# One decoder layer on one core: a norm factor spread later, one empty step ahead of a small product, a weight split moved into the last boundary loop, one more idle product

## The chip, the cores and the metric

The kernel runs on one core of a Trainium2 chip. Time is device microseconds (us) of one execution, the median over several runs. Below, PE is the matrix engine (TensorE), PEld its weight loads, DVE the vector engine, ACT the scalar engine, POOL GpSimd, and SP the engine that issues most of the transfers. The time before the change is 914.59 us, the median of 3 runs (913.2 to 915.72).

## The reference

One hybrid decoder layer over 512 tokens of width 1024, all in float32, in three sub-layers with a norm before and after each:

```
x = x + 0.5 * post1(swiglu1(pre1(x)))            # 1024 -> 2 x 2816 -> 1024
q, k, v, u = split(pre2(x) @ w_mix_in)           # 4 x 512 columns
a = dilated_attention(q, k, v)                   # 8 heads x 64
s = s5_mixer(u)                                  # 32 groups x 16 channels, 64 states
x = x + post2(concat(a, s) @ w_mix_out)
x = x + 0.5 * post3(swiglu2(pre3(x)))
```

`rms_norm` divides each token by the root of its mean square, so a sub-layer's first products can run on the unscaled input, and the factor r of each token is multiplied in when the product is read. The S5 mixer needs small parameter tensors that depend on the weights alone: powers of `a_bar`, `b_bar`, and short convolution kernels made from `b` and `c`.

## The kernel before, in words

**Tiling.** x and the hidden tensors lie transposed, channels on the 128 partitions and 512 tokens along the row. A weight tile of 128 x 1024 (512 KB) gives one product of a `[128, 1024]` block of weights with x: eight steps k over the 1024 channels. For precision every float32 operand is split into a high and a low part (`whi`, `wlo` of a weight, `xh`, `xl` of x), and each step is three matmuls of 512 columns (`mm3`). ACT makes the high part (a cast), DVE or POOL the low part (a subtraction). Weights go through three raw buffers (`wraw`) and four pairs of halves.

**Stages.** `run` chains ffn1 (span 0 to about 350), a boundary, mix (to about 600), a boundary, and ffn2. A boundary ends one sub-layer (its last products `yt`, the post norm, the residual) and starts the next (pre norm, and the first four products `first`), in two halves of 256 tokens each: the first loop over k prepares and multiplies half 0, the second half 1. `prep` makes y, x, `xh`, `xl` of one k and half on DVE and ACT, `begin` issues its 12 matmuls.

**ffn1.** Ahead of it PE runs five products of zeros (`idle`, plain float32, each as two matmuls). `products(f)` makes the gate and up products (`gu`) of block f, 24 matmuls each; `hidden(f)` reads them with r, applies silu and splits the result into `ah`, `al`. Blocks 0 to 7 are done so; `outp(0)` then multiplies them with the output weights (`yo`), of which the first two outputs m = 0 and 1 leave out the last block and take it up at the end. The factor r comes late: `sums` adds up squares with four tiny matmuls (`st`), DVE scales (`nv`), POOL takes the power (`r`), and `spread` copies r to all partitions with four matmuls against the identity (`rp`), which ACT copies to `rs`. The table `between` says at which k of which product this is issued.

**The parameters of S5 as a side job.** `ssm_params` is a generator. `step()` runs it to its next `yield`; the tables `other` and `between`, and `part` in `outp(0)`, call it after certain k, so its DVE, ACT and PE work is issued between the large products. Near its end it transposes `gb` in eight groups (`w1t`, four transposes each), copies each to a buffer `w1s` (ACT), and writes it to memory (`w1d`, SP); then makes `cz` (two tiles `pp`, cleared by POOL, filled by four ACT instructions at the line with `scale=1.0 - 2.0 * q`), then multiplies `cz` and `gb` into `kb` in two halves, copies that to `kt`, and transposes `kt` (`kc`). `gt`, `ut`, `w1s` and `kt` all come from one ring of four `[128, 512]` buffers.

**What sets the order.** Every engine runs its own list in order. The framework orders the list from the program's order and its own estimates; instructions through `self.fix` keep the program's order among themselves (all of PE's products here, most of DVE's in a boundary). A wait in front of an instruction holds up all behind it on its engine. SP issues transfers in order, and a load waits there until its buffer is free.

**`soon`.** `mix_soon` loads the weights of mix's first product and splits them into a room of its own, by one ACT cast and one DVE subtraction of 128 x 1024. The boundary calls it when it comes to the place `soon and k == ...`.

Of the kernel before, what the change touches and what calls it, by code (L numbers as in the profile page):

```python
# [17 lines left out]
P = 128  # L18
S = 512
D = 1024  # L20
KD = D // P
# [24 lines left out]
class Layer:  # L46
    def __init__(self, ctx, tc, a):
        self.tc, self.nc, self.a = tc, tc.nc, a
        pool = lambda n, b, **k: ctx.enter_context(tc.tile_pool(name=n, bufs=b, **k))
        self.cst = pool("cst", 1)  # L50
        self.big = pool("big", 6)
        self.wp = pool("wp", 2)
        self.tp = pool("tp", 4)
        self.sp = pool("sp", 2)
        self.ps = pool("ps", 8, space=PSUM)
        self.dr = pool("dr", 1, space=DRAM)
        nc = self.nc

        self.sw = self.tmp("sw")[:, :52 + P]
        nc.scalar.dma_start(out=self.sw, in_=a["smalls"])  # L60
        warm = self.tmp("warm")[:, :HT]
        nc.vector.memset(warm, 0.0)

        idle = self.bank("idle")
        for _ in range(5):
            self.mm(idle[:, :HT], lhsT=warm[:, :P], rhs=warm, start=True, stop=True)
        self.ident = self.cst.tile([P, P], F32, name="ident")
        make_identity(nc, self.ident)
        self.ones = self.cst.tile([P, 2], F32, name="ones")
        nc.vector.memset(self.ones, 1.0)  # L70
        self.mhalf = self.cst.tile([P, 4], F32, name="mhalf")
        nc.scalar.activation(out=self.mhalf, in_=self.ones[:, :1].to_broadcast([P, 4]), func=AF.Copy, scale=-0.5)
        self.mone = self.cst.tile([P, 4], F32, name="mone")
        nc.vector.memset(self.mone, -1.0)
        self.sm = self.cst.tile([P, 52], F32, name="sm")
        self.gh = self.cst.tile([P, 52], F32, name="gh")
# [78 lines left out]
    def fix(self, i):  # L155
        return self.tc.keep_in_program_order(i)
# [136 lines left out]
    def boundary(self, y, tail, ipost, half, inext, chunks, wide=None, soon=None):  # L293
# [40 lines left out]
        def prep(h, k, fix=lambda i: i):  # L334
            t = y(k)[:, hs[h]]
            xk = self.x(k)[:, hs[h]]
            fix(nc.vector.scalar_tensor_tensor(out=t, in0=t, scalar=self.g(ipost, k, half), in1=rr[h],
                                               op0=ALU.mult, op1=ALU.mult))
            fix(nc.vector.tensor_tensor(out=xk, in0=t, in1=xk, op=ALU.add))
            self.split(xh(k)[:, hs[h]], xl(k)[:, hs[h]], xk, self.g(inext, k), fix)  # L340
            if wide:
                fix(nc.scalar.activation(out=t, in_=xk, func=AF.Copy, scale=self.g(inext, k)))
            self.sq_acc(acc2[:, hs[h]], xk, k == 0, nc.gpsimd)

        def begin(h, k):
            for i in range(len(w)):
                self.mm3(o[i][:, hs[h]], w[i][0][:, k], w[i][1][:, k], xh(k)[:, hs[h]], xl(k)[:, hs[h]],
                         k == 0, k == KD - 1)
# [24 lines left out]
        late = []  # L373
# [18 lines left out]
        for k in range(KD):  # L392
            if k > 1:
                prep(0, k, fx if k > 5 else lambda i: i)
            begin(0, k)
            if soon and k == 2:
                soon()
            if k == 2:
                post[1][0](late, fix=fx)
            if k == 4:  # L400
                rr[1] = post[1][1]()
        for k in range(KD):
            prep(1, k)
            begin(1, k)
            if not wide and k == 3:
                pre[0][0](fixp=fx)
            if not wide and k == 6:
                pre[0][1]()
# [7 lines left out]
    def ffn(self, n, first, scope):  # L416
# [6 lines left out]
        o0, _, r, late = first  # L423
# [3 lines left out]
        nfirst = len(o)  # L427
# [3 lines left out]
        step = lambda: next(hook, None)  # L431
        other = {1: step, 3: step, 5: step}
        between = {(nfirst, 0): {}, (nfirst, 1): {}, (nfirst + 1, 0): {1: lambda: late[0](fixp=self.fix), 3: step, 5: step},
                   (nfirst + 1, 1): {1: late[1], 3: step, 5: step}}
        halves = iter([(f, i) for f in range(nfirst, NSTD[0]) for i in range(2)][len(self.ahead):])

        def ahead():
# [511 lines left out]
    def ssm_params(self, scope):  # L949
# [181 lines left out]
        czf = [t.rearrange("p n g c -> p n (g c)") for t in cz]  # L1131
        kt = self.tmp("kt")
        yield
        kb = self.bank("kb")
        for n4 in range(4):
            o = kb[:, n4 * P:(n4 + 1) * P]
# [98 lines left out]
    def mix_soon(self):  # L1235


        room = self.b16("soon", F32R).rearrange("p (i k) c -> p i (k c)", i=4)
        self.soon = self.load(self.a["wmi"][0], (KD, P), [room[:, 0], room[:, 1]])

    def mix_chunks(self):
        return [self.a["wmi"][c] for c in range(12, 16)]
# [398 lines left out]
```

## Time and profile before

| what | value |
|---|---|
| median of 3 runs | 914.59 us (913.2 to 915.72) |
| profiled execution, its own time | 914.35 us |
| its span, first to last instruction | 912.5 us |
| mean granted PE clock | 0.996 |
| busy: PE, DVE, ACT, POOL | 897.3, 663.1, 456.0, 217.1 us |
| bytes moved | 118.37 MB, mean 130 GB/s |

A row of the timeline gives the start in us, the duration, the engine, the line, the operation with output and inputs, and in brackets the idle time before it and what ended that. A matmul's duration is modelled to the end of its pipeline; how fast PE goes is read from the distance of two starts. Products of 512 columns start 0.227 us apart at full rate, those of 256 columns 0.114 us. Matmuls of plain float32 and transposes show as two records each.

### The profile page before, as it was taken

To read this page: it belongs to the slowest core of one execution; us is meant where nothing else is said; L and a number is where in the kernel's file an instruction comes from. 1 tells how busy PE (TensorE), PEld (TensorE's weight loads), DVE (VectorE), ACT (ScalarE), POOL (GpSimd) and SP (SyncE) were. 2 spreads that over 40 slices of the span, in tenths; PEclk is the share of its full clock that TensorE was granted. 3 is DMA by queue.
4 is the path that set the end of the run, shared out by engine and by line. 5 is a ranking of instruction groups with operands and counts; after the bars stand their busy time and mean duration, and the time that the engine had idled before them with its cause. 6 is when DMAs were issued, how large, how long until landed. Compare 5 with 4: busy or idle time off the path is not lost.

```text
span 912.5 us, 15703 instructions
## 1 busy us (share of the span) xinstructions
PE 897.3 (98%) x6314; PEld 807.0 (88%) x6314; DVE 663.1 (73%) x1065; ACT 456.0 (50%) x705; POOL 217.1 (24%) x130
## 2 busy tenths in 40 slices
PE   9999899999999999999999999999999999999996
PEld 7788688998899989988777789999899989998995
DVE  6998576765578565958989587996279658965966
ACT  7262573553355543535637465774456414541542
POOL 0253202342323224430000023513122212231211
PEclk9999999999999999999999999999999999999999
DMA  8224479664522153184221443363422412342322
GB/s 276 95 70 127 150 253 266 153 177 149 146 93 82 53 189 94 48 251 148 84 91 57 141 162 108 89 219 129 150 93 95 160 70 93 116 139 72 113 93 92
DMA packets 52760, 118.37 MB, mean 130 GB/s; under 512 B 8176, under 2 KB 11504, under 8 KB 52080
## 3 DMA queue, kind: packets, MB, share of 16 engines
q1 hardware_dynamic: 48928, 109.55, 36.5%
q0 software_dynamic: 2176, 4.19, 2.9%
q10 hardware_dynamic: 1584, 3.63, 1.1%
q8 instruction: 49, 0.80, 0.4%
q14 instruction: 23, 0.19, 0.1%
HBM read 107.66 MB, written 18.09 MB: 138 GB/s over the span
## 4 chain that ended last, share of the span: by engine, by line
PE 82%; DVE 11%; DMA 2%; issue 2%; ACT 2%; POOL 1%; SPq 0%; POOLq 0%; DVEq 0%; ACTq 0%
PE yo L164 22%; PE wx L164 20%; PE wq L164 10%; PE yt L164 6%; PE wy L164 5%; PE first L164 4%; PE prj L164 4%; PE prv L164 2%; DVE pp L964 2%; PE mo L164 2%; DVE wlo L139 2%; PE ys L164 1%; PE st L164 1%; DMA w1d<-w1s 1%; PE gl L164 1%
## 5 line engine op out<-in xcount | busy, mean ns | idle before, releaser
L137 ACT CAST whi<-wraw 128x1024 fp32r<-128x1024 f32 (+5 forms) x122 | 117.9, 971 | 139.3 <-PE yo L164 60.0
L139 POOL TENSOR_TENSOR wlo<-wraw,whi 128x1024 fp32r<-128x1024 f32 (+1 forms) x37 | 96.6, 2611 | 286.3 <-ACT whi L137 274.9
L139 DVE TENSOR_TENSOR wlo<-wraw,whi 128x1024 fp32r<-128x1024 f32 (+5 forms) x85 | 103.2, 1220 | 64.6 <-ACT whi L137 60.2
L164 PE MATMUL wx<-tq,whi 128*128 128x256 f32 (+1 forms) x817 | 141.6, 276 | 0.0
L164 PEld LDWEIGHTS wx<-tq,whi 128*128 128x128 f32 x817 | 122.8, 188 | 0.1
L139 DVE TENSOR_TENSOR wlo<-wsum,whi 128x1024 fp32r<-128x1024 f32 x68 | 82.8, 1219 | 48.4 <-ACT whi L137 48.4
L164 PE MATMUL wx<-tq,wlo 128*128 128x256 f32 x408 | 112.6, 276 | 0.0
L137 ACT CAST whi<-wsum 128x1024 fp32r<-128x1024 f32 x68 | 71.2, 1048 | 76.9 <-PE yo L164 25.8
L139 POOL TENSOR_TENSOR wlo<-wx,whi 128x1024 fp32r<-128x1024 f32 x16 | 46.1, 2882 | 197.3 <-ACT whi L137 161.4
L164 PEld LDWEIGHTS wx<-tq,wlo 128*128 128x128 f32 x408 | 76.6, 188 | 0.0
L164 PE MATMUL yo<-whi,ah 128*128 128x512 f32 x144 | 56.8, 395 | 0.0
L164 PE MATMUL yo<-whi,al 128*128 128x512 f32 x144 | 56.2, 390 | 0.0
L164 PE MATMUL yo<-ah,whi 128*128 128x512 f32 x144 | 56.1, 390 | 0.0
L164 PE MATMUL yo<-wlo,ah 128*128 128x512 f32 x144 | 56.1, 390 | 0.0
L164 PE MATMUL yo<-al,whi 128*128 128x512 f32 x144 | 56.1, 389 | 0.0
L164 PE MATMUL yo<-ah,wlo 128*128 128x512 f32 x144 | 56.0, 389 | 0.0
L164 PE MATMUL gu<-xh,whi 128*128 128x512 f32 x112 | 45.3, 405 | 0.0
L164 PE MATMUL gu<-xl,whi 128*128 128x512 f32 x112 | 44.1, 393 | 0.0
L164 PE MATMUL gu<-xh,wlo 128*128 128x512 f32 x112 | 44.0, 393 | 0.0
L164 PE MATMUL first<-xh,whi 128*128 128x256 f32 (+1 forms) x144 | 43.3, 300 | 0.6 <-ACT xh L186 0.6
L164 PE MATMUL first<-xl,whi 128*128 128x256 f32 (+1 forms) x144 | 43.3, 301 | 0.3 <-DVE xl L187 0.2
L164 PE MATMUL first<-xh,wlo 128*128 128x256 f32 (+1 forms) x144 | 42.3, 294 | 0.0
(310 smaller groups left out, 2499.3 us busy)
## 6 DMA issues: line engine op xcount, KB each, us to landing
wraw<-w1i SPq DMA_DIRECT2D x28, 512.0 KB, 3.9
wraw<-w2i SPq DMA_DIRECT2D x24, 512.0 KB, 3.6
wraw<-w2o SPq DMA_DIRECT2D x18, 512.0 KB, 4.5
wraw<-wmi SPq DMA_DIRECT2D x12, 512.0 KB, 4.0
wx<-w2i SPq DMA_DIRECT2D x10, 512.0 KB, 3.5
wraw<-w1o SPq DMA_DIRECT2D x8, 512.0 KB, 3.6
c<-w2i POOLq DMA_DIRECT2D x8, 512.0 KB, 7.6
wsum<-c SPq DMA_DIRECT2D x8, 512.0 KB, 4.2
```

The lines of the kernel that those rows point to most:

```text
L137: fix(self.nc.scalar.copy(out=hi, in_=raw))
L139: fix(eng.tensor_tensor(out=lo, in0=raw, in1=hi.bitcast(F32), op=ALU.subtract))
L164: i = self.nc.tensor.matmul(*a, **k)
L964: tt = lambda o, x, y, op: V.tensor_tensor(out=o, in0=x, in1=y, op=op)
```

## The change

Four edits:

- `between`: r is spread after k = 4 of the second product of block 2 in place of after k = 1, nine matmuls later, and that product calls one `step()` in place of two. So every later piece of `ssm_params` is issued one call later.
- `ssm_params`: one more empty `yield` ahead of `kb`, so `kb` and what follows are issued one further call later.
- `boundary` and `mix_soon`: `soon()` is called at k = 5 of the second loop in place of k = 2 of the first, and its two instructions now keep the program's order.
- `__init__`: a sixth idle product, of 128 columns.

```
         for _ in range(5):
             self.mm(idle[:, :HT], lhsT=warm[:, :P], rhs=warm, start=True, stop=True)
+        self.mm(idle[:, :P], lhsT=warm[:, :P], rhs=warm[:, :P], start=True, stop=True)
...
             if k > 1:
                 prep(0, k, fx if k > 5 else lambda i: i)
             begin(0, k)
-            if soon and k == 2:
-                soon()
...
         for k in range(KD):
             prep(1, k)
+            if soon and k == 5:
+                soon()
             begin(1, k)
...
-                   (nfirst + 1, 1): {1: late[1], 3: step, 5: step}}
+                   (nfirst + 1, 1): {4: late[1], 6: step}}
...
         kt = self.tmp("kt")
         yield
+        yield
         kb = self.bank("kb")
...
-        self.soon = self.load(self.a["wmi"][0], (KD, P), [room[:, 0], room[:, 1]])
+        self.soon = self.load(self.a["wmi"][0], (KD, P), [room[:, 0], room[:, 1]], fix=self.fix)
```

The order of PE around the first half of `kb` (`kb` is the output, `gb` and `pp104`, `pp105` the inputs; numbers count the tiles). Before:

```order
L164 MATMUL gu_1081<-xl_100,whi_1028 128x512
L164 MATMUL gu_1081<-xh_99,wlo_1029 128x512
L164 MATMUL kb_1088<-gb_703,pp104_1060 32x128 x4
L164 MATMUL kb_1088<-gb_704,pp105_1061 32x128 x4
L164 MATMUL gu_1081<-xh_99,whi_1028 128x512
```

and with the change:

```order
L165 MATMUL yo_1115<-al_249,whi_1068 128x512
L165 MATMUL yo_1115<-ah_248,wlo_1069 128x512
L165 MATMUL kb_1122<-gb_710,pp104_1080 32x128 x4
L165 MATMUL kb_1122<-gb_711,pp105_1081 32x128 x4
L165 MATMUL yo_1115<-ah_248,whi_1068 128x512
```

The half stood after k = 1 of the last `gu` product; it now stands after k = 1 of the first `yo` product, 24 matmuls of 512 columns further on.

The order of ACT from the weights of the first `yo` product to the copy `kt` (`w1s<-w1t` copy transposes out, `pp104` and `pp105` are `cz`, `gt` and `ah` belong to `hidden`). Before:

```order
L137 CAST whi_1076<-wraw_1075 128x1024
L1119 COPY w1s_990<-w1t_985 128x512
L1119 COPY w1s_1010<-w1t_1005 128x512
L456 ACTIVATE gt_1019<-gt_1019 128x512
L137 CAST whi_1203<-wraw_1202 128x1024
L183 CAST ah_247<-ut_1020 128x512
L1119 COPY w1s_1045<-w1t_1040 128x512
L1129 ACTIVATE pp104_1060<-pp4_341 64x16x16 x2
L1129 ACTIVATE pp105_1061<-pp4_341 64x16x16 x2
L137 CAST whi_1314<-wraw_1313 128x1024
L1143 COPY kt_1068<-kb_1088 128x512
```

and with the change:

```order
L138 CAST whi_1068<-wraw_1067 128x1024
L1130 ACTIVATE pp104_1080<-pp4_342 64x16x16 x2
L1130 ACTIVATE pp105_1081<-pp4_342 64x16x16 x2
L1120 COPY w1s_983<-w1t_978 128x512
L1120 COPY w1s_1003<-w1t_998 128x512
L457 ACTIVATE gt_1012<-gt_1012 128x512
L138 CAST whi_1172<-wraw_1171 128x1024
L184 CAST ah_248<-ut_1013 128x512
L1120 COPY w1s_1038<-w1t_1033 128x512
L1120 COPY w1s_1058<-w1t_1053 128x512
L138 CAST whi_1315<-wraw_1314 128x1024
L457 ACTIVATE gt_1107<-gt_1107 128x512
```

`cz` stood behind three copies to `w1s`; it now stands ahead of four. The copy to `kt` follows three rows after the last one shown.

The order of DVE around the subtraction for `soon` in the boundary from ffn1 to mix (`rp_3783` serves half 0 of the tokens, `rp_3956` and, with the change, `rp_3952` half 1; `nv_4093` and `nv_4089` are the first step of half 0's next norm factor). Before:

```order
L339 TENSOR_TENSOR x_98<-y_246,x_98 128x256
L139 TENSOR_TENSOR soon_3903<-wraw_3904,soon_3903 128x1024
L187 SCALAR_TENSOR_TENSOR xl_3587<-x_98,sm_96,xh_3586 128x256
L337 SCALAR_TENSOR_TENSOR y_246<-y_246,gh_97,rp_3783 128x256
L187 SCALAR_TENSOR_TENSOR xl_3587<-x_98,sm_96,xh_3586 128x256
```

and with the change:

```order
L338 SCALAR_TENSOR_TENSOR y_247<-y_247,gh_98,rp_3952 128x256
L340 TENSOR_TENSOR x_99<-y_247,x_99 128x256
L140 TENSOR_TENSOR soon_4118<-wraw_4119,soon_4118 128x1024
L188 SCALAR_TENSOR_TENSOR xl_3588<-x_99,sm_97,xh_3587 128x256
L226 TENSOR_SCALAR nv_4089<-st_4086 128x2
L188 SCALAR_TENSOR_TENSOR xl_3588<-x_99,sm_97,xh_3587 128x256
L226 TENSOR_SCALAR nv_4201<-st_4198 128x2
L140 TENSOR_TENSOR wlo_4230<-wraw_4228,whi_4229 128x1024
```

The subtraction left the middle of half 0's work and now stands ahead of the last two `xl` of half 1.

More of the change, by code (lines that the diff above doesn't have):

```diff
@@ L66, in __init__ @@
             self.mm(idle[:, :HT], lhsT=warm[:, :P], rhs=warm, start=True, stop=True)
+        self.mm(idle[:, :P], lhsT=warm[:, :P], rhs=warm[:, :P], start=True, stop=True)
         self.ident = self.cst.tile([P, P], F32, name="ident")
@@ L395, in boundary @@
             begin(0, k)
-            if soon and k == 2:
-                soon()
             if k == 2:
@@ L403, in boundary @@
             prep(1, k)
+            if soon and k == 5:
+                soon()
             begin(1, k)
@@ L433, in ffn @@
         between = {(nfirst, 0): {}, (nfirst, 1): {}, (nfirst + 1, 0): {1: lambda: late[0](fixp=self.fix), 3: step, 5: step},
-                   (nfirst + 1, 1): {1: late[1], 3: step, 5: step}}
+                   (nfirst + 1, 1): {4: late[1], 6: step}}
         halves = iter([(f, i) for f in range(nfirst, NSTD[0]) for i in range(2)][len(self.ahead):])
@@ L1133, in ssm_params @@
         yield
+        yield
         kb = self.bank("kb")
@@ L1238, in mix_soon @@
         room = self.b16("soon", F32R).rearrange("p (i k) c -> p i (k c)", i=4)
-        self.soon = self.load(self.a["wmi"][0], (KD, P), [room[:, 0], room[:, 1]])
+        self.soon = self.load(self.a["wmi"][0], (KD, P), [room[:, 0], room[:, 1]], fix=self.fix)
     def mix_chunks(self):
```

## The prediction

> **What bounds the kernel now.** I read the busy times first, then what PE waited for, then the timeline of PE around each wait, then the engines behind it.
>
> ```profile
> PE 897.3 (98%) x6314; PEld 807.0 (88%) x6314; DVE 663.1 (73%) x1065; ACT 456.0 (50%) x705; POOL 217.1 (24%) x130
> ```
>
> PE works without a break nearly everywhere, so an edit counts only by the idle time of PE that it removes or makes, or by the rate at which PE runs. The waits of PE, with total, count and longest in us:
>
> ```profile
> PE kb L164 <- issue: 2.3, 1, 2.3
> PE rp L164 <- POOL r L227: 1.6, 1, 1.6
> PE kb L164 <- ACT pp L1129: 0.5, 1, 0.5
> ```
>
> The change touches all three, and the start and the boundary, whose shorter gaps come below. The largest, in PE's timeline:
>
> ```profile
> 98.95 0.39 PE L164 MATMUL gu<-xh,wlo 128*128 128x512 f32 x1
> 101.61 0.43 PE L164 MATMUL kb<-gb,pp 128*32 128x128 f32 x8 [2.27 <-issue]
> 102.52 1.38 PE L164 MATMUL kb<-gb,pp 128*32 128x128 f32 x24 [0.48 <-ACT pp L1129]
> 103.84 0.80 PE L164 MATMUL gu<-xh,whi 128*128 128x512 f32 x1
> 107.85 1.08 PE L164 MATMUL kb<-gb,pp 128*32 128x128 f32 x32
> 108.86 0.50 PE L164 MATMUL gu<-xh,whi 128*128 128x512 f32 x1
> 110.35 0.40 PE L164 MATMUL yo<-ah,whi 128*128 128x512 f32 x1
> ```
>
> PE could have gone on at 99.18 (0.23 after the start of the last `gu`) and stands until 101.61. The name "issue" says that the trace saw no releaser; ACT's rows show one:
>
> ```profile
> 100.19 0.59 ACT L1119 COPY w1s<-w1t 128x512 f32<-128x512 f32 x1 [2.29 <-DMA w1d<-w1s]
> 100.67 1.71 ACT L1129 ACTIVATE pp<-pp 64x256 f32<-64x256 f32 x4
> ```
>
> ACT waited for a buffer of the ring until a `w1d` write had landed, and only then made `cz`: its first two instructions end near 101.5, where `kb` starts, the last two near 102.4, where the second part starts. The wait leaves a second loss, in the granted clock (the number before the DMA share):
>
> ```profile
> 102.00:103.00 1.00, 0.52 (x16) 0.51 (x17) 0.00 (x0) 0.98 (x2) 0.00 (x0) 0.86 0.96 363
> 103.00:106.00 3.00, 3.00 (x24) 2.23 (x16) 1.83 (x2) 0.45 (x1) 0.00 (x0) 0.50 0.41 96
> ```
>
> PE runs at 0.50 for about 3 us behind the gap.
>
> **kb: what the move is worth.** Standing: 103.84 - 99.18 = 4.66 us between products, of which a half of `kb` needs 1.01 when nothing is late (107.85 to 108.86), so 3.65 are lost. Half clock: the twelve products from 103.84 to 107.85 take 4.01, while six at full rate take 1.49 (108.86 to 110.35), twelve 2.98; 1.03 are lost. Together 4.7 us.
>
> Is the new place late enough? `kb` stands 24 products further on, 24 x 0.227 = 5.4 us. PE gets there at 99.18 + 5.4 - 1.5 (the gain of `rp`, below) = 103.1. Even in ACT's old order `cz` was done at 102.4. In the new one it precedes four `w1s` copies, so its limit is POOL's clearing:
>
> ```profile
> 90.45 0.99 POOL L1126 MEMSET pp<- 128x512 f32 x2
> ```
>
> 91.4 plus four times 0.43 gives 93.2: ten us of cover. What is late next? The four copies that `cz` overtook go through the ring; the last pair waits for the landing of the pair before.
>
> ```profile
> DMA to landing us min/median/max: 2.5/4.6/4.8
> ```
>
> By my estimate the pair after `cz` is copied by 94.3, lands by 99 (4.6 later), and the last pair is copied by 99.8. Behind it on ACT stand the weights of the third `yo` product (cast by 101, needed by PE at about 115), `gt` and `ah` of block 7, then `kt`. The last pair's write is queued on SP behind a load and lands at about 104.5, which frees the ring's slot for `kt`. The second half of `kb` ends on PE at about 106.4, `kt` is copied by 107.2, and `kc` stands 15 products behind, at 109.8: 2.6 us of cover. If that cover is gone, PE loses what is missing one for one. All eight accumulator banks that PE takes here were emptied at least 3 us earlier in this reckoning. Bounds of the term: 0 (the wait moves along) to 4.7. I take 4.7, since every cover that I can name is positive.
>
> **rp.**
>
> ```profile
> 37.93 0.39 PE L164 MATMUL gu<-xh,wlo 128*128 128x512 f32 x1
> 39.88 1.16 PE L164 MATMUL rp<-ident,r 128*128 128x128 f32 x8 [1.57 <-POOL r L227]
> 38.79 1.03 POOL L227 TENSOR_TENSOR r<-nv,mhalf 128x4 f32<-128x4 f32 x1 [3.67 <-DVE pp L964]
> ```
>
> POOL has r at 39.82. Nine products more are 9 x 0.227 = 2.04 us, so PE wants r at 38.16 + 2.04 = 40.20 and no longer waits: 1.57 at most in this execution, with 0.3 of cover. `rs` is then some 0.5 us later, and DVE places six more `ssm_params` instructions ahead of the first `gt`:
>
> ```profile
> 44.89 1.09 DVE L964 TENSOR_TENSOR pp<-pp,pp 128x256 f32<-128x256 f32 x3
> 45.89 0.68 DVE L455 TENSOR_TENSOR gt<-first,rs 128x512 f32<-128x512 f32 x1
> ```
>
> At 1.09 for three, `gt` goes from 45.9 to about 48. It frees accumulators that block 4 takes 66 products after `rp`, at about 54 by my estimate (39.9 + 66 x 0.227 is 54.9, less what PE gains). Nothing waits. The one `step()` fewer changes places, not work. I take 1.5; bounds 0 to 2.04.
>
> **soon.** Half 0 of the boundary is where DVE is behind PE:
>
> ```profile
> 366.56 1.04 ACT L137 CAST soon<-wraw 128x1024 fp32r<-128x1024 f32 x1
> 368.68 1.21 DVE L139 TENSOR_TENSOR soon<-wraw,soon 128x1024 fp32r<-128x1024 f32 x1
> 373.44 0.28 PE L164 MATMUL first<-xh,wlo 128*128 128x256 f32 x1
> 373.87 0.71 PE L164 MATMUL rp<-ident,p 128*128 128x128 f32 x4
> 377.16 0.28 PE L164 MATMUL first<-xh,whi 128*128 128x256 f32 x1
> 377.57 0.39 PE L164 MATMUL first<-xl,whi 128*128 128x256 f32 x1
> 378.98 0.38 PE L164 MATMUL first<-xh,whi 128*128 128x256 f32 x1
> 379.56 0.38 PE L164 MATMUL first<-xl,whi 128*128 128x256 f32 x1 [0.20 <-DVE xl L187]
> ```
>
> Three steps from product to product are 0.43, 0.41 and 0.58 in place of 0.114: 0.32 + 0.30 + 0.47 = 1.1 us. The 1.21 us on DVE ahead of them go away, so all three can. At the new place, DVE and PE stood so:
>
> ```profile
> 386.23 0.48 DVE L187 SCALAR_TENSOR_TENSOR xl<-x,sm,xh 128x256 fp32r<-128x256 f32 x1
> 388.40 0.28 PE L164 MATMUL first<-xl,whi 128*128 128x256 f32 x1
> 387.62 0.48 DVE L187 SCALAR_TENSOR_TENSOR xl<-x,sm,xh 128x256 fp32r<-128x256 f32 x1 [0.58 <-ACT xh L186]
> 389.70 0.38 PE L164 MATMUL rp<-ident,r 128*128 128x128 f32 x2
> ```
>
> `xl` of k = 6 was 1.7 us ahead of its product. DVE gains about as much as PE, and 1.21 now stand in between: 0.0 to 0.5 of cover. The load behind `soon` on SP, so far issued at 369.93 as its buffer came free, now goes at about 386.5, and its cast stood at 396.48, so about 6 us remain after 4 of landing.
>
> ```profile
> 369.93 0.33 SPq L143 DMA_DIRECT2D wraw<-wmi  x1
> 396.48 1.05 ACT L137 CAST whi<-wraw 128x1024 fp32r<-128x1024 f32 x1
> ```
>
> I take 0.9; bounds -0.5 (the 1.21 stand in the way after all, less the small cover, and only part is regained) to 1.1.
>
> **The idle product.**
>
> ```profile
> 1.22 4.64 PE L164 MATMUL idle<-warm 128*128 128x256 f32 x10 [1.22 <-DVE pp L972]
> 6.47 0.80 PE L164 MATMUL first<-xh,whi 128*128 128x512 f32 x1 [0.61 <-ACT xh L186]
> 9.98 0.63 PE L164 MATMUL first<-xl,whi 128*128 128x512 f32 x1
> 11.18 0.39 PE L164 MATMUL first<-xh,wlo 128*128 128x512 f32 x1
> ```
>
> Ten matmuls of 256 columns take 4.64, two of 128 about 0.46; they end by 6.3 inside the gap of 0.61, so they cost nothing. The first products stand 0.43 apart until about 10.4 and 0.227 from there: half rate. A shorter gap may end this sooner, by up to nine products x 0.2 = 1.8 us, but then PE only meets r at 39.82 again; at most 0.3 is left over. I take 0.
>
> [...]
>
> **The sum.** 4.7 + 1.5 + 0.9 + 0 = 7.1 us. The profiled execution took 914.35, its span 912.5, and lies 0.2 under the median of 914.59. Span 905.4, execution 907.25, median 907.5: 0.8% faster. Less than 0.3% (2.7 us) can hardly be told from no change here.
>
> **The rivals.**
>
> *The start gets longer (chance 0.10).* The wait at `rp` hid up to 1.57 us of a slow start; without it a start whose half-rate spell is 3 us longer, as long as the spell at `kb`, costs seven products x 0.2 = 1.4. For it: 0.3 of cover is all that is left. Against: the idle product works the other way. 908.9. [...]
>
> *The wait was not for cz (0.07).* The trace says "issue" for 2.27. If PE stood there for a reason of its own, it stands at the new place too, with the half clock behind it: 7.1 - 3.65 - 1.03 = 2.4 gained, 912.2. Against: `cz` ends within 0.1 us of both starts.
>
> *The ring decides, a little (0.06) or wholly (0.04).* `kt` needs the slot of the last `w1s` pair. From a `kt` more than 2.6 us late, PE waits at `kc`. One round trip of 4.6 late gives 2.0 of wait, and 1 more if the clock halves: 909.5 to 910.5. To be slower than before takes three round trips, 13.8 late: 11.2 of wait and 1 of half clock against 7.1 gained, 919.7. For it: before, ACT and DVE both stood for `w1d` writes here. Against: ring use at each `hidden` is lower now, since two copies less stand ahead of block 5's.
>
> *soon only moves its wait (0.05).* 1.2 us at k = 6 and 7 in place of the 1.1 removed: no gain here, 908.4 to 908.9.
>
> *The forecast (0.68).* Its own range, with noise of about 0.7 us as in the three runs, is 906 to 909.
>
> The lower end of all is 4.7 + 2.04 + 1.1 = 7.8, 906.8, less 1 of noise: 905.8. The upper end takes in the short ring case: 910.5. Faster: 0.68 + 0.10 + 0.06 + 0.05 = 0.89; within 0.3%: 0.07; slower: 0.04.
>
> **What would show it.** In the changed profile: no wait at `kb`, and the granted clock at 1.00 from 99 to 107; no wait at `rp` of block 2, or one under 0.3; steps between `first` products in the boundary all near 0.114 at k = 6 and 7 of half 0 and k = 0 of half 1; PE busy still about 897 in a span near 905. The prediction is wrong if a wait stands at `kc` or at a `yo` product's weights, if the half clock returns, or if PE waits for `xl` at k = 6 or 7 of half 1.

## The result, and the profile after

The changed kernel takes 910.53 us, the median of 22 executions (906.28 to 914.98), against 913.58 for the kernel before in 22 executions beside it: a ratio of 0.9962, with a 95% interval of 0.9948 to 0.9976. That is 3.0 us less, where 7.1 were forecast. The median is of little use here, since the 22 times fall into two groups: ten from 906.3 to 908.3, where the forecast of 907.5 lies, and twelve from 910.2 to 915.0. The profiled execution, 911.97 with a span of 910.1, is of the upper group.

PE's busy time and its longest waits in the changed kernel, with total, count and longest in us:

```profile
PE 896.8 (99%) x6316; PEld 808.4 (89%) x6316; DVE 668.8 (73%) x1065; ACT 455.6 (50%) x705; POOL 215.3 (24%) x130
```

```profile
PE wx L165 <- DVE kp L720: 2.6, 1, 2.6
...
PE rp L165 <- POOL r L228: 0.2, 1, 0.2
```

Both rows of `kb` are gone, and of the wait at `rp` 0.2 is left. Where PE stood and then ran at 0.50 before, and in half 0 of the boundary, the busy times by stretch now read as follows (PE's busy time is the second number; the granted clock stands ahead of the last two):

```profile
101.00:104.00 3.00, 3.00 (x41) 2.20 (x40) 2.90 (x4) 1.73 (x3) 0.00 (x0) 1.00 0.89 307
104.00:107.00 3.00, 3.00 (x41) 2.22 (x40) 1.37 (x3) 0.59 (x1) 1.49 (x1) 1.00 0.95 305
...
370.00:390.00 20.00, 20.00 (x147) 18.51 (x146) 12.86 (x26) 10.16 (x21) 9.46 (x11) 1.00 0.53 165
```

So the places that the change aimed at do what was forecast. Matching the products of the two traces in their order shows how far the changed kernel is ahead at the same product (start before, less start after; the value that holds behind the place named):

| behind | ahead by, us |
|---|---|
| the tenth product | 1.5 |
| `rp` of block 2 | 2.8 |
| `kb` and `kc` | 7.4 |
| half 0 of the boundary | 8.9 |
| mix | 7.8 |
| the stall at 784.87, its first product | 5.1 |
| the same stall, six us later | 3.3 |
| the last product | 2.6 |

What is new is one stall in the last stage. PE's timeline, and the stretches behind it:

```profile
782.05 0.28 PE L165 MATMUL wq<-xh,wlo 128*128 128x256 f32 x1
784.87 0.50 PE L165 MATMUL wx<-tq,whi 128*128 128x256 f32 x2 [2.55 <-DVE kp L720]
```

```profile
785.00:787.00 2.00, 2.00 (x11) 2.00 (x12) 1.97 (x3) 0.29 (x1) 0.00 (x0) 0.59 0.74 242
787.00:789.00 2.00, 2.00 (x13) 2.00 (x12) 1.49 (x2) 0.77 (x1) 0.00 (x0) 0.56 0.08 29
```

PE stands for 2.55 us and then runs near half clock for almost 4. By the table this costs 7.8 - 3.3 = 4.5 us, and about so far apart are the medians of the two groups, 907.7 and 912.1. The rows of SP, DVE and POOL tell how it comes about. In this stage a `pair` of blocks takes seven block products; DVE forms sums of weight blocks (the additions at L654) and splits them (L140), and POOL splits two blocks of each pair, `h12 = cut(a12, True)` and `cut(a22, True)`. The timeline of SP, DVE and POOL in the changed kernel:

```profile
768.86 0.37 SPq L624 DMA_DIRECT2D wsum<-w2i  x1
770.02 0.34 SPq L144 DMA_DIRECT2D wraw<-w2o  x1
...
774.06 1.23 DVE L654 TENSOR_TENSOR wsum<-wraw,wsum 128x1024 f32<-128x1024 f32 x1 [1.22 <-DMA wsum<-w2i]
...
775.27 3.41 POOL L140 TENSOR_TENSOR wlo<-wx,whi 128x1024 fp32r<-128x1024 f32 x1 [11.26 <-ACT whi L138]
...
776.34 4.56 DVE L654 TENSOR_TENSOR wsum<-wsum,wx 128x1024 f32<-128x1024 f32 x2
...
780.65 2.48 POOL L140 TENSOR_TENSOR wlo<-wraw,whi 128x1024 fp32r<-128x1024 f32 x1 [1.97 <-ACT whi L138]
...
780.82 3.40 DVE L140 TENSOR_TENSOR wlo<-wraw,whi 128x1024 fp32r<-128x1024 f32 x1
784.14 0.68 DVE L720 TENSOR_TENSOR kp<-wx,kp 128x512 f32<-128x512 f32 x1
```

The load of 768.86 landed late, so DVE began its first addition 1.22 late. Two additions then met POOL's first split and took 4.56; where they start ahead of it (below) they take 2.35. The next split of DVE started 0.17 behind POOL's second one and took 3.40 in place of 1.22. `kp`, the addition that frees the accumulators `wx` that PE wants, came after it.

### The profile page after: what moved, and what is told of

The parts are those of the page before. It is cut to its first block, busy times and chain, and to the rows that moved or that the text cites. A ratio compares the mean times of both kernels' runs of the same rounds, so it can differ in the third digit from the quotient of the medians.

```text
span 910.1 us, 15705 instructions
## 1 busy us (share of the span) xinstructions
PE 896.8 (99%) x6316; PEld 808.4 (89%) x6316; DVE 668.8 (73%) x1065; ACT 455.6 (50%) x705; POOL 215.3 (24%) x130
## 4 chain that ended last, share of the span: by engine, by line
PE 88%; DVE 5%; ACT 1%; issue 1%; POOLq 0%; POOL 0%; DVEq 0%; ACTq 0%
PE yo L165 22%; PE wx L165 21%; PE wq L165 10%; PE gu L165 6%; PE yt L165 6%; PE wy L165 5%; PE prj L165 4%; PE first L165 4%; PE prv L165 2%; PE mo L165 2%; PE ys L165 1%; PE st L165 1%; PE gl L165 1%; PE pt L1225 1%; PE sc L165 1%
## 5 line engine op out<-in xcount | busy, mean ns | idle before, releaser
L140 POOL TENSOR_TENSOR wlo<-wraw,whi 128x1024 fp32r<-128x1024 f32 (+1 forms) x37 | 96.0, 2595 | 284.4 <-ACT whi L138 260.0
L165 PE MATMUL wx<-tq,whi 128*128 128x256 f32 (+1 forms) x817 | 143.6, 279 | 2.6 <-DVE kp L720 2.6
L140 DVE TENSOR_TENSOR wlo<-wraw,whi 128x1024 fp32r<-128x1024 f32 (+5 forms) x85 | 103.3, 1222 | 55.4 <-ACT whi L138 52.4
L140 DVE TENSOR_TENSOR wlo<-wsum,whi 128x1024 fp32r<-128x1024 f32 x68 | 82.9, 1220 | 44.1 <-ACT whi L138 44.1
L140 POOL TENSOR_TENSOR wlo<-wx,whi 128x1024 fp32r<-128x1024 f32 x16 | 45.6, 2847 | 202.0 <-ACT whi L138 189.9
L654 DVE TENSOR_TENSOR wsum<-wsum,wx 128x1024 f32<-128x1024 f32 x23 | 42.4, 1872 | 0.2
```

The costliest lines, as they stand in the source:

```text
L140: fix(eng.tensor_tensor(out=lo, in0=raw, in1=hi.bitcast(F32), op=ALU.subtract))
L165: i = self.nc.tensor.matmul(*a, **k)
L654: add = lambda x, z, t: V.tensor_tensor(out=t, in0=x, in1=z, op=ALU.add)
```

## The experiments

Twelve runs were made (one repeats the changed kernel, and the kernel without the idle matmul was run twice), in three groups, each group on one chip beside runs of the kernel before, whose median was 914.62, 913.27 and 913.40. Times are medians in us; ratios are to the kernel before, with a 95% interval.

### The changed kernel again, and the four ways to change the stall

**Once more**, with no edit.

> The changed kernel once more. Up to 780 us its trace is 7.8 us ahead of the one before; at 784.87 PE stands for 2.55 us (wx behind DVE's kp) and then runs at half clock for about 4 us, and ends only 2.4 ahead. Theory A (one late load): in that execution the w2i load of a wsum buffer landed 5.1 us after its issue, where the others take 3.5 to 3.8; DVE's add started 1.2 late and DVE's next split then met POOL's split and took 3.40 us in place of 1.22. Then the stall comes and goes from execution to execution: the times fall into two groups, about 907.5 without it and 911 to 913 with it, and a profile near 907.5 shows no wait at kp. Rival B (a place that is always short now): every execution has a wait at that place, and the two groups come from something else, so a profile near 907.5 would show the wait as well. Rival C: the groups come from the half-rate spell at the beginning, some 2 us longer or shorter; then a slow execution has its first full-rate product near 10 us and a fast one near 7.

910.40 (906.84 to 911.73, six executions; 0.9945, 0.9925 to 0.9964): 906.84 and 907.50 on one side, 909.53 to 911.73 on the other. The profile, of 911.27, has the stall again (PE waits 2.7 behind `kp`), again behind a late load (5.2 us). Its half-rate spell at the beginning ended at 7.4, as in the first profile of the upper group (7.3), which rules out C. A profile of an execution of the lower group was not obtained for this kernel, so A is not separated from B by this run alone.

**Without POOL in the pairs:**

```
- h12 = cut(a12, True)
+ h12 = cut(a12)
- times(X, h22 if ahead else cut(a22, True), tq[2], False)
+ times(X, h22 if ahead else cut(a22), tq[2], False)
```

> The changed kernel with both splits of each pair that POOL does (a12 and a22) done by DVE. DVE gets some 2.4 us more work per pair of 19 us, and never works beside POOL there. Theory A (the stall is the meeting of DVE and POOL behind a late load): no stall is left even where the load is late, DVE's splits and adds all take 1.22 us, and the times are one group near 907.5. Rival B (DVE is simply short of time there, whoever it meets): with more work on DVE the stall is as long or longer, in more executions, 911 to 915. Rival D (a late load is enough by itself): two groups as before.

907.88 (907.18 to 909.34, five executions; 0.9926, 0.9912 to 0.9940): one group. In its trace the same load is later than ever (5.9 us), DVE's timeline shows a wait of 2.00 for it, and yet:

```profile
775.46 1.22 DVE L654 TENSOR_TENSOR wsum<-wraw,wsum 128x1024 f32<-128x1024 f32 x1 [2.00 <-DMA wsum<-w2i]
...
781.14 1.22 DVE L140 TENSOR_TENSOR wlo<-wraw,whi 128x1024 fp32r<-128x1024 f32 x1
```

PE's waits in that kernel:

```profile
PE wx L165 <- DVE kp L720: 0.3, 1, 0.3
```

Every one of DVE's splits and additions takes 1.22 and PE waits 0.3. So a late load alone does not stall PE, nor does more work on DVE; the meeting with POOL is needed. B and D fall.

**Without the added idle matmul:**

```
- self.mm(idle[:, :P], lhsT=warm[:, :P], rhs=warm[:, :P], start=True, stop=True)
```

> The changed kernel without its added idle matmul (five of 512 columns are left). Counted by products, the changed kernel's trace is 1.5 us ahead by the tenth product, since its half-rate spell ends near 7.3 us in place of 10.4, and r comes 0.7 earlier. Theory I (the idle matmul closes the gap ahead of the first product, and the clock therefore rises earlier): without it the spell lasts to about 10.4 again, and the kernel takes 0.7 to 1.5 us more, 908.2 to 909 without the stall. Rival (the spell's end moves by itself from execution to execution): the median stays at about 907.5 without the stall, and the spell's end is not bound to this edit.

The five that are left have 256 columns each, not 512. 907.86 (907.12 to 909.59, five executions; 0.9921, 0.9907 to 0.9936): faster than the changed kernel, and no stall. Theory I falls: the half-rate spell ended at 7.3 without the idle matmul as well. The kernel with the empty step alone, which has no sixth idle matmul either, also had it end at 7.2. Of all the traces only the one before had a spell to 10.4.

Why no stall? The timeline of SP, DVE and POOL at the same pair:

```profile
770.76 0.37 SPq L623 DMA_DIRECT2D wsum<-w2i  x1
...
774.65 1.22 DVE L653 TENSOR_TENSOR wsum<-wraw,wsum 128x1024 f32<-128x1024 f32 x1
...
776.92 2.35 DVE L653 TENSOR_TENSOR wsum<-wsum,wx 128x1024 f32<-128x1024 f32 x2
...
777.18 4.36 POOL L139 TENSOR_TENSOR wlo<-wx,whi 128x1024 fp32r<-128x1024 f32 x1 [11.26 <-ACT whi L137]
...
779.84 2.78 DVE L139 TENSOR_TENSOR wlo<-wraw,whi 128x1024 fp32r<-128x1024 f32 x1 [0.56 <-ACT whi L137]
...
782.56 2.40 POOL L139 TENSOR_TENSOR wlo<-wraw,whi 128x1024 fp32r<-128x1024 f32 x1 [1.03 <-ACT whi L137]
```

DVE's additions started ahead of POOL's split, kept their 2.35, and POOL's took 4.36. The load was not late. What the transfer engines did in the 3.5 us behind the issue of that load (packets, MB and share of the 16 engines' time for each queue, and the load's us to landing), first in the changed kernel:

```profile
q1 hardware_dynamic: 309, 0.69, 57.4%
q8 instruction: 1, 0.02, 1.8%
...
wsum<-w2i SPq DMA_DIRECT2D x1, 512.0 KB, 5.1
```

and in the kernel without the idle matmul:

```profile
q1 hardware_dynamic: 304, 0.66, 56.3%
...
wsum<-w2i SPq DMA_DIRECT2D x1, 512.0 KB, 3.6
```

One packet of 16 KB of instructions, which takes about 1 us (0.88 to 1.45 over the 49 of the changed kernel's trace), stands among the load's packets in the one and not in the other. Between such fetches PE runs 111 to 147 matmuls in the changed kernel's last stage, 127.6 in the mean of eleven, each with its weight load; the list of packets in the trace gives their times. The whole trace has 49 of them for 6316 matmuls and as many weight loads, 258 to a packet and near the 255 of the last stage (2 x 127.6), so they are taken for PE's; the trace does not name the engine. No wait of PE in this stage is put down to a fetch, but the load with such a packet among its own landed after 5.1 us, the one without after 3.6. The added idle product is two matmul records (6316 in place of 6314; the transposes show as one record each, `w1t` as 32 for 32), so by this estimate every later packet is fetched two records earlier in PE's work. This is called theory F in the expectations that follow.

The fourteen traces bear F out at this pair, with one point left open. In all of them the load is issued at the same place of PE's work, behind 5406 matmuls without the idle ones. In the five traces with 10 idle records the fetch starts 3.5 to 5.7 us behind the issue, and the load lands after 3.5 or 3.6; in the seven traces with 12 records it starts 1.2 to 3.4 behind, and the load lands after 3.9 to 5.9. That point is the size: two records of 256 columns are only 0.23 us of PE's work, two steps of 0.114. Counted in all of PE's matmul records, idle ones too, this fetch never starts before the 5427th. In three traces (the two with 22 idle records and the one with 12 and no POOL in the pairs) it starts there or two records on, in the others up to 39 records later. Why a difference of 0.23 in when it could start so often decides whether it falls among the load's packets or behind them was not shown.

**The same, a second time.**

> The changed kernel without its added idle matmul, a second time: its five executions so far were 907.1 to 909.6, none with the stall, where the changed kernel has it in about half of 28. Theory F (two records fewer leave the fetch behind the load): no execution above 910. Rival (chance: five of five at one half has 3%): about half of them at 911 to 913.

907.02 (905.63 to 908.57, five executions; 0.9930, 0.9915 to 0.9945). Ten of ten executions without the idle matmul are below 910, and its second profile shows no wait at `kp`.

**As many records, no added work:**

```
- for _ in range(5):
+ for _ in range(4):
      self.mm(idle[:, :HT], lhsT=warm[:, :P], rhs=warm, start=True, stop=True)
- self.mm(idle[:, :P], lhsT=warm[:, :P], rhs=warm[:, :P], start=True, stop=True)
+ for _ in range(2):
+     self.mm(idle[:, :P], lhsT=warm[:, :P], rhs=warm[:, :P], start=True, stop=True)
```

> The changed kernel with the idle matmul taken away again and one of the five of 256 columns cut into two of 128: the columns of the kernel without it, but 12 matmul records ahead of the first product, as many as in the changed kernel. Theory F (the number of records sets where the 16 KB fetch falls against the w2i load): the fetch runs 2.5 to 3.1 us behind that load's issue, and the stall is back in about half of the executions: two groups, 907.5 and 911 to 913, median 909 to 911. Rival (the added work or the shorter gap at the beginning was the cause): one group at 907.0 to 907.9, as in the two kernels without the idle matmul, and the fetch 4.4 or more behind the load.

910.45 (906.33 to 913.13, twelve executions; 0.9957, 0.9939 to 0.9975), in two groups again: five from 906.3 to 908.5, seven from 910.2 to 913.1. Its profile (913.13) has the fetch 3.4 behind the issue (2.5 to 3.1 were expected), the load landing after 5.5 us, and the stall. PE's longest waits there:

```profile
PE wx L166 <- DVE kp L721: 2.9, 1, 2.9
PE rp L166 <- POOL r L229: 1.8, 1, 1.8
```

The columns are those of the kernel without the idle matmul; only the records differ. F holds in that the records decide, and the work or the gap at the beginning is not the cause.

**Ten records more:**

```
- for _ in range(5):
-     self.mm(idle[:, :HT], lhsT=warm[:, :P], rhs=warm, start=True, stop=True)
- self.mm(idle[:, :P], lhsT=warm[:, :P], rhs=warm[:, :P], start=True, stop=True)
+ for _ in range(11):
+     self.mm(idle[:, :P], lhsT=warm[:, :P], rhs=warm[:, :P], start=True, stop=True)
```

> The changed kernel with its idle matmuls in eleven pieces of 128 columns in place of five of 256 and one of 128: the same columns less nothing and the same 4.7 us of work ahead of the first product, but 22 matmul records in place of 12. Theory F: PE's instructions are fetched in pieces of 16 KB, a piece for about 128 matmuls with their weight loads, so ten more records ahead bring every later fetch 1.1 us earlier against the work. In the two stalled traces the fetch (about 1 us on one transfer engine) ran 2.5 to 3.1 us behind the issue of the late w2i load, in the traces without the stall 4.4 to 4.7 behind it, after the load had landed. With the fetch due ahead of the load's packets, the load lands in 3.5 to 3.8 again and the times are one group near 907.5. Rival (the load is late for another reason): two groups, 907.5 and 911 to 913, as in the changed kernel.

911.90 (909.09 to 914.57, twelve executions; 0.9983, 0.9971 to 0.9995). The number that was expected is missed: there is no group at 907.5. The stall has left its place, as F said, but stands at another. At the old pair the fetch now falls at 773.05, 0.15 behind the issue of the load at 772.90. That load still lands after 4.7, so the step of the expectation that such a fetch is harmless is wrong too, but no stall follows there. At an earlier pair, where output weights are loaded beside it as well, the fetch falls 3.0 behind the issue and the load lands after 5.2:

```profile
678.49 0.37 SPq L623 DMA_DIRECT2D wsum<-w2i  x1
...
683.73 1.22 DVE L653 TENSOR_TENSOR wsum<-wraw,wsum 128x1024 f32<-128x1024 f32 x1 [1.26 <-issue]
...
690.29 2.52 POOL L139 TENSOR_TENSOR wlo<-wraw,whi 128x1024 fp32r<-128x1024 f32 x1 [1.93 <-ACT whi L137]
...
690.50 3.39 DVE L139 TENSOR_TENSOR wlo<-wraw,whi 128x1024 fp32r<-128x1024 f32 x1
```

The picture is that of the changed kernel, about 90 us earlier, with 0.21 in place of 0.17 between POOL and DVE.

**Ten records more, and no POOL in the pairs.** Both edits above together.

> Eleven idle matmuls of 128 columns, as in idle_small, and both of POOL's splits of each pair done by DVE. With POOL's splits that start gave 911.9, nearly every execution slow, and a stall of 2.6 us at another pair (the load issued at 678.49, the fetch 3.0 behind it). Theory A and F together: the load of that pair is late again, but DVE meets nobody, so no PE wait at kp above 0.5 and one group near 907.5 to 908.5. Rival (the late load alone, or the start, costs the time): 911 to 912.5 again.

908.71 (906.97 to 911.02, six executions; 0.9947, 0.9929 to 0.9965), 3.2 below the same start with POOL. In its trace the load at 679.25 is late (4.7 us) and DVE goes on at its pace:

```profile
684.07 1.22 DVE L653 TENSOR_TENSOR wsum<-wraw,wsum 128x1024 f32<-128x1024 f32 x1 [0.84 <-DVE gp L660]
...
689.75 1.22 DVE L139 TENSOR_TENSOR wlo<-wraw,whi 128x1024 fp32r<-128x1024 f32 x1
```

PE has no wait at `kp`. A and F hold together here: the load is late at this start too, and with POOL out of the pairs PE does not stall. The one execution at 911.02 is not explained.

### The parts of the change alone

**The idle matmul alone**, on the kernel before (the added line and nothing else).

> The kernel before with the added idle matmul as its only change. Forecast: nothing, 913.3. Theory F (two more records move the fetch ahead of the w2i load's last packets): the stall of 2.6 us with its half clock comes in about half of the executions, two groups, 913 and 917, median 1 to 4 us above before. Rival (the idle matmul helps the start): 912 to 913, one group.

917.10 (912.89 to 921.34, twelve executions; 1.0039, 1.0022 to 1.0057): 3.7 slower. Only two of the twelve are below 915. The profile is of one of these, 914.19: there the fetch falls 3.3 behind the issue, the load lands after 3.9, and there is no stall. So the stall in the others was not seen in a trace of this kernel; that it is their cause is argued from the kernels above, not shown.

**The empty step alone:**

```
          yield
+         yield
          kb = self.bank("kb")
```

> The kernel before with the empty step ahead of kb as its only change. By the forecast's term (3.65 standing and 1.03 at half clock): 4.7 us less, 908.9 on the scale of 913.6, no wait at kb and the clock at 1.00 behind it. If the stall in the last stage goes with how early PE comes there, some of its executions show it too (about 4.4 us more, 913), and its times fall into two groups; if the stall needs another part of the change, its times are one group near 908.9.

913.08 (910.10 to 914.88, twelve executions; 0.9981, 0.9970 to 0.9992): 1.5 faster, not 4.7. In the trace the term itself is right: no wait at `kb`, and from behind `rp` to behind `kb` this kernel gains 4.6 on the one before. But another wait is larger:

```profile
PE rp L164 <- POOL r L227: 3.1, 1, 3.1
```

The half-rate spell is short here, so PE comes to `rp` earlier, and r comes at 40.36, 0.5 later than before. The larger wait costs only these 0.5. So this execution is 4.1 ahead behind `kb`; mix takes 0.5 of it and a longer wait at `yt` (1.1 in place of 0.2) 0.9, and it ends 2.7 ahead. It took 911.67, 1.4 less than the median of the twelve, and what the others lost was not seen: that the empty step alone gives 1.5 and not 4.7 is explained in part only.

**The edit at r alone:**

```
-                  (nfirst + 1, 1): {1: late[1], 3: step, 5: step}}
+                  (nfirst + 1, 1): {4: late[1], 6: step}}
```

> The kernel before with the spread of r nine products later as its only change. The forecast's sum took 1.5 for it and added it to 4.7 for kb: then 913.3 less 1.5, 911.8. The other reading (the wait at kb ends at a time that ACT's transposes and their transfers set, so that PE, coming sooner, only stands longer there): no gain, 913.0 to 913.6, the wait at rp 0.3 to 1.2 and the one at kb as much longer.

908.81 (907.57 to 909.74, six executions; 0.9947, 0.9930 to 0.9963): 4.6 faster, where both theories had 0 to 1.5. All PE waits of 0.2 and more in its trace, but for the one ahead of the first idle product:

```profile
PE first L164 <- DVE xl L187: 0.9, 4, 0.3
PE ys L164 <- issue: 0.7, 1, 0.7
PE yt L164 <- DVE so L187: 0.2, 1, 0.2
PE rp L164 <- POOL r L227: 0.2, 1, 0.2
```

There is no wait at `kb`. This edit also takes one `step()` away, which moves `kb` twelve products on by itself, and that was enough. Whether the empty step adds anything once this edit is there, and what the spread would give with both steps kept, was not tried.

**The change without the edit at r** (that line back as it was).

> The changed kernel with the spread of r at its old place, nine products earlier. The forecast's term: 1.5 us more than the changed kernel, 909.0 where the stall of the last stage is absent, with a wait of 1.6 at rp. Since the kernel with the empty step alone stood 3.1 us at rp (its half-rate spell at the beginning was short, and r came no earlier), the other reading is: PE waits 2.0 to 3.1 at rp, and where the half clock follows that gap another 1 to 1.5, so 909.5 to 912, in a wide group and not in two narrow ones.

911.66 (908.73 to 919.76, twelve executions; 0.9982, 0.9963 to 1.0001), a wide group, as the other reading said; the stall of the last stage widens it too, so it is the trace and not the times that decides between the two readings. Its profile is that of the slowest execution, 919.76, which also has the stall at `kp` and a wait of 1.6 in mix, at the products `sc`. Its wait at `rp`, and the stretches behind:

```profile
PE rp L165 <- POOL r L228: 3.4, 1, 3.4
```

```profile
40.00:42.00 2.00, 1.73 (x9) 1.74 (x9) 2.00 (x20) 0.00 (x0) 0.21 (x1) 0.50 0.00 0
42.00:44.00 2.00, 2.00 (x7) 1.61 (x7) 1.97 (x12) 1.60 (x2) 0.00 (x0) 0.50 0.00 0
44.00:46.00 2.00, 2.00 (x7) 1.57 (x6) 2.00 (x5) 0.27 (x1) 0.00 (x0) 0.56 0.01 4
```

The half clock lasts from 40 to past 45. The kernel with the empty step alone, behind a gap of 3.1:

```profile
42.00:44.00 2.00, 2.00 (x11) 1.64 (x10) 1.97 (x13) 1.49 (x2) 0.00 (x0) 1.00 0.00 0
```

Full clock. In the idle matmul's kernel a gap of 2.4 had half clock behind it, to past 42. So by my estimate the gap at `rp` costs from 1.6 (before) to some 6 us (3.4, and about half of the 5.3 at half clock), as the execution has it.

**The change with `soon` at its old place:**

```
+             if soon and k == 2:
+                 soon()
              if k == 2:
...
-             if soon and k == 5:
-                 soon()
...
- self.soon = self.load(self.a["wmi"][0], (KD, P), [room[:, 0], room[:, 1]], fix=self.fix)
+ self.soon = self.load(self.a["wmi"][0], (KD, P), [room[:, 0], room[:, 1]])
```

> The changed kernel with mix's first split at its old place. The forecast's term: 0.9 us more, 908.4 where the stall is absent, with the three steps of 0.4 to 0.6 between products in half 0 of the boundary. Rival: the section behind it is paced by its transfers (ys waits there for them), and then nothing is lost in the end, 907.5. Either way the stall of the last stage stays in some of its executions, 911 to 913.

910.69 (908.15 to 915.22, twelve executions; 0.9973, 0.9956 to 0.9990): six from 908.2 to 909.7, six from 911.7 to 915.2. The lower group stands about 1 above the lower groups of the changed kernel and 1.9 above the kernel without the idle matmul in the same set of runs. Its trace is 7.7 ahead of the kernel before both at the beginning and at the end of half 0, where the changed kernel goes from 7.4 to 8.9, so the term is there, and by the medians it is not lost again. Its profile is of the lower group, though its load was late too (4.7). The timeline of DVE and POOL there:

```profile
781.97 1.21 DVE L140 TENSOR_TENSOR wlo<-wraw,whi 128x1024 fp32r<-128x1024 f32 x1
...
782.14 3.30 POOL L140 TENSOR_TENSOR wlo<-wraw,whi 128x1024 fp32r<-128x1024 f32 x1 [2.31 <-ACT whi L138]
```

Here DVE is 0.17 ahead of POOL, takes 1.21, and POOL pays with 3.30; in the changed kernel it was 0.17 behind and took 3.40, and POOL 2.48. No stall in the one, 4.5 us in the other. In these two pairs of rows the one that starts second is the slow one. So it is in all others: in the last stage of the fourteen traces 94 pairs of such instructions of 128 x 1024, a split or an addition of DVE and a split of POOL, start within 0.5 us of each other. In the 76 where DVE is ahead, by 0.03 or more, DVE takes 1.21 to 1.23 and POOL 2.97 to 4.36; in the 18 where POOL is ahead, by 0.03 or more, DVE takes 3.13 to 3.44 and POOL 2.38 to 2.83. Most of these slow ones cost PE nothing. The five stalls in the traces are the five places where a split of 3.39 or 3.40 stands right ahead of `kp`, and each followed a load that landed after 5.1 to 5.5 us; three loads that landed after 3.9 to 4.8 us in kernels with POOL's splits were followed by none.

## Why the prediction was right, and where it was wrong

**How close it came.** The change is faster, and the lower group lies where the forecast of 907.5 was. But the median, 910.53, stands at the far end of the range (905.8 to 910.5), and that end was set for a ring that frees its buffers late. What brought the median there is a stall in the last stage that no rival named. That the range reached so far is luck.

**The idle product is the step that failed.** "... so they cost nothing. ... I take 0." In the trace before it did fit into a gap of 0.61. The spell did end early, but it did so without the added product as well (7.3). What was left out is that two more records on PE come ahead of all its later instructions; in the seven traces with 12 records ahead the 16 KB fetch starts 1.2 to 3.4 us behind the issue of the load, in the five with 10 it starts 3.5 to 5.7 behind. Measured: the changed kernel (twice) and the one with its five products cut anew have 12 records ahead and medians of 910.4 to 910.5, with 22 of 40 executions above 910; the kernel with 10 records has 907.0 and 907.9, with none of ten above. Added to the kernel before it costs 3.7. In place of 0 the term is a loss of about 3. That is most of the 4.1 us by which the gain of 3.0 falls short of 7.1. The step gave it a gain of up to 0.3 and no loss at all. That records and not work decide is shown by the kernel with the products cut anew, and that the stall needs POOL by the two kernels without it there. That the late load comes from the fetch rests on their going together in the traces; why some executions of one kernel stall and others do not stays open, since no lower-group execution of the changed kernel itself was traced.

**The rest of the sum held.** Without the idle product the change gives 913.27 - 907.02 = 6.3 and 914.62 - 907.86 = 6.8, against 7.1. That this is so close is partly luck. In the trace of the changed kernel `rp` gives 2.8, `kb` 4.6 and `soon` 1.3, together 8.7, and 0.9 is lost in mix: two misses that offset each other.

**kb, 4.7.** The size in a trace was right (4.6 in the kernel with the empty step alone, and 7.4 - 2.8 = 4.6 from the table above), and so were the covers: no wait at `kc`, at `yo`'s weights or for a slot of the ring. The wait went with `cz`: none is left at the new place. The attribution was not tested in the forecast: the edit at r, which moves `kb` too, gave 4.6 alone, and the empty step alone 1.5.

**rp, 1.5, bounds 0 to 2.04.** Too small, and the bound was wrong: behind `rp` the changed kernel is 2.8 ahead. The term was read from one execution, whose long spell at the beginning hid half of the wait, and it took r as fixed at 39.82. In the changed kernel's trace r comes at 39.1, in the others anywhere from 38.8 to 41.1. In three other traces with r at its old place PE stood 2.4, 3.1 and 3.4, in two of them with half clock behind it. The nine products take 2.04 of this; what remained in the changed kernel was 0.2 and 0.5, and in the one with its five products cut anew, where r came last of all, 1.8. So the cover of 0.3 does not hold in every execution.

How `rp` and `kb` share their gain also depends on the execution. In the kernel with the idle matmul alone PE came to `kb` late, after half clock behind `rp`, and stood there only 0.22 and 0.48:

```profile
100.76 0.43 PE L165 MATMUL kb<-gb,pp 128*32 128x128 f32 x8 [0.22 <-issue]
101.67 0.86 PE L165 MATMUL kb<-gb,pp 128*32 128x128 f32 x24 [0.48 <-ACT pp L1130]
```

Together the two edits gave 5.0 to 5.5 (6.3 to 6.8 less the 1.3 at `soon`) against 6.2.

**soon, 0.9.** Right in kind, a little small: 8.9 - 7.4 = 1.5 in half 0 of the boundary, since the step right behind each of the three long ones (0.21 or 0.22 in place of 0.114) became short too. In half 1 a sign of being wrong that the forecast had named did come, though small: at k = 6 PE waits for `xl`. DVE and PE there:

```profile
379.07 0.48 DVE L188 SCALAR_TENSOR_TENSOR xl<-x,sm,xh 128x256 fp32r<-128x256 f32 x1
...
379.37 0.28 PE L165 MATMUL first<-xh,whi 128*128 128x256 f32 x1
379.60 0.38 PE L165 MATMUL first<-xl,whi 128*128 128x256 f32 x1
379.82 0.28 PE L165 MATMUL first<-xh,wlo 128*128 128x256 f32 x1
```

Two steps of 0.23 and 0.22 in place of 0.114 cost 0.2, which leaves 1.3. Mix takes another 0.9 of the lead, 0.4 of it at `ys`, its output products, where PE waits 0.5 before and 0.9 after; the rest was not followed up.

**The rivals.** A longer start (908.9) did not come: the spell ended by 7.5 in every new trace. The wait that was not for `cz` and the ring did not come either. The case that came, half clock behind a new stall in the last stage, was not among them; the signs to watch named the half clock, but at `kb`.

**A version that is faster than both** is the change without its idle product: 0.9921 and 0.9930 of the kernel before, about 3 us less than the changed kernel.

## What to carry to other kernels

An instruction that fits into an idle gap may be free only where it stands: here one that fit into a gap of 0.61 us put two records ahead of all that follows on its engine, went with fetches 1.2 to 3.4 us behind the issue of a load in place of 3.5 to 5.7, and cost about 3 us. Read a wait from more than one execution before a bound is set by it, above all a wait behind a phase whose length varies. Two engines that must not meet should be kept apart by the program, not by 0.2 us of timing: here a split of DVE took 3.40 beside POOL's in place of 1.22, and moving POOL's splits to DVE took the stall away and cost nothing that shows (907.88, beside 907.86 without the idle matmul). Both together were not tried.

## What was not expected of the hardware

- Where a fetch of 16 KB of instructions, about 1 us or more, fell 0.2 to 3.1 us behind the issue of a 512 KB load of `w2i` with a load of `w2o` issued 1.1 or 1.2 behind it, the load landed after 4.7 to 5.9 us in place of 3.5 or 3.6. At 3.5 and more it did not. At 3.3 and 3.4 both were seen (3.9 and 5.5). At the stage's first pair, where the other load goes 2.3 to 2.9 ahead, the link is loose: a fetch 3.3 behind went with landings from 3.7 to 5.4.
- A DVE split of 1.22 us that starts 0.17 behind one of POOL takes 3.40; 0.17 ahead of it 1.21, and POOL's goes from 2.40 to 3.30.
- A gap of 3.1 us in PE's work left the granted clock at 1.00, while gaps of 2.4, 2.55 and 3.4 were followed by 3 to 5 us near 0.50.
